# Moving the activation tiles of a decoder kernel by 64 bytes in on-chip memory

## The chip, the cores and the metric

The kernel runs on one core of one Trainium2 chip. The metric is the device time of one execution in microseconds (us). Three runs of the kernel before gave 1953.02, 1953.22 and 1953.27 us, a median of 1953.22.

## The reference

A decoder trunk of two layers, for 512 tokens of 1024 features in float32. Every sub-layer is wrapped in two norms: `x = x + w * norm(f(norm(x)))`, with `w` = 1/2 for the feed-forward sub-layers and 1 for the mixers.

```
ffn(h)   = (silu(h @ w_gate) * (h @ w_up)) @ w_down        # 1024 -> 2816 -> 1024, four times
conv(h)  = (b * causal_conv3(c * u)) @ w_out               # b, c, u = split(h @ w_in), layer 0
k, v     = split(norm(x) @ w_kv)                           # after layer 0
attn(h)  = norm((softmax(q1 k1) - lam * softmax(q2 k2)) v) @ w_o   # 8 heads, causal, layer 1
```

Layer 0 is ffn, conv, ffn; layer 1 is ffn, attn, ffn.

## The kernel before

Features lie on the 128 partitions, tokens along the free dimension; the residual stream `x` is one tile of 8 x 512 floats in each partition. All large products are made of three float32r matmuls (L128 to L130): weights and activations are each split into a high and a low part, and `hi*hi + hi*lo + lo*hi` is summed in PSUM.

```
nc.tensor.matmul(acc, wh, ah, start=first and j == 0, stop=False)
nc.tensor.matmul(acc, wh, al, start=False, stop=False)
nc.tensor.matmul(acc, wl, ah, start=False, stop=last and j == n - 1)
```

The second argument is the stationary operand, which TensorE loads first (LDWEIGHTS, 128 columns); the third is the moving operand, which it then streams. In the projections (`products`, called by `projects`) the weight part is stationary, 128 x 128, and the activation part is streamed: 512 columns for all tokens, or 256 for one half of the tokens. Halves are used around the end of a sub-layer (`closing` and the `head` of the next one), where the norm of one half runs while TensorE works on the other. In two places the roles are swapped: the last down projection (`ByTokens`, L339 to L341, sums named `d_acc`) and the values of attention (`values`, L567 to L569, sums named `v_acc`) hold 128 x 128 of an activation part still and stream 512 columns of a weight part. The scores of attention (L602) multiply tiles from the weight pools with each other: `pair_of_units("kq")` holds the parts of the queries and keys of one head.

A weight unit (`unit`, L107) is loaded by SyncE's queue into a `raw` tile of 4096 bytes per partition, ScalarE copies it to the high part `whi` (L113) and VectorE subtracts to get the low part `wlo` (L114). There are 2 raw tiles and 7 pairs of parts; units are prepared ahead and wait for a free pair.

Nothing in the kernel names an address. Memory of a partition is handed out to the pools in the order in which they are created, and within a pool to its tiles one after the other, each rounded up to 32 bytes. The pools that matter, with the start addresses of the built program, and what is left after dividing by 256:

| pool, in the order before | tiles, bytes per partition | start before, remainder | start after, remainder |
|---|---|---|---|
| `const` | 15 constants, 3136 together | 16512, 128 | 16512, 128 |
| `xpool` | the residual stream, 16384 | 19648, 192 | 19712, 0 |
| `apool` | 40 activation tiles, 2048 each | 36032, 192 | 36096, 0 |
| `mpool` | 2 large tiles, 8224 each (attention weights, conv) | 117952, 192 (second: 224) | 183552, 0 (second: 32) |
| `wraw` | 2 raw weight tiles, 4096 each | 134400, 0 | 175360, 0 |
| `wsp` | 7 + 7 weight parts, 4096 each | 142592, 0 | 118016, 0 |
| `tpool` | temporaries, 1024 and 2048 each | 199936, 0 | 200000, 64 |
| `rpool` | rows of the norms | 219008, 128 | 219072, 192 |

All slices that a matmul takes of an `apool` or `wsp` tile start at a multiple of 512 bytes from the tile's start, so they have the tile's remainder. Before, the streamed operand of a projection has the remainder 192 and the stationary one 0; in the swapped products it is the other way round.

Of the kernel before, what the change touches and what calls it, by code (L numbers as in the profile page):

```python
# [17 lines left out]
P = 128  # L18
# [5 lines left out]
NH = 8  # L24
HD = 64
EPS = 1e-6
CHUNKS = [(0, 7), (7, 14), (14, 22)]
LAST_CHUNKS = [(0, 8), (8, 16), (16, 22)]
HALVES = [(0, 256), (256, 512)]
# [13 lines left out]
def yoco_kernel(ctx: ExitStack, tc, i, out):  # L43
# [2 lines left out]
    const = ctx.enter_context(tc.tile_pool(name="const", bufs=1))  # L46
    xpool = ctx.enter_context(tc.tile_pool(name="xpool", bufs=1))
    apool = ctx.enter_context(tc.tile_pool(name="apool", bufs=5 * NK))
    mpool = ctx.enter_context(tc.tile_pool(name="mpool", bufs=1))
    wraw = ctx.enter_context(tc.tile_pool(name="wraw", bufs=RAW))  # L50
    wsp = ctx.enter_context(tc.tile_pool(name="wsp", bufs=WUNITS))
    tpool = ctx.enter_context(tc.tile_pool(name="tpool", bufs=1))
    small = ctx.enter_context(tc.tile_pool(name="small", bufs=4))
    rpool = ctx.enter_context(tc.tile_pool(name="rpool", bufs=1))
# [15 lines left out]
    ps = ctx.enter_context(tc.tile_pool(name="ps", bufs=6, space=PSUM))  # L70
    pst = ctx.enter_context(tc.tile_pool(name="pst", bufs=2, space=PSUM))

# [1 line left out]
    nc.scalar.preload_act_table_set("abs_reciprocal_sqrt_and_small")  # L74
    halves = {}
    for n in (D, 2 * HD):
# [10 lines left out]
    gsub = const.tile([P, 1], F32, name="gsub")  # L87
    nc.scalar.dma_start(gsub, i["gsub"])

# [1 line left out]
    x = xpool.tile([P, NK, S], F32, name="x")  # L91

    def load_x(k, n, t):
# [8 lines left out]
        return hi, lo  # L102

    def unit(src, n, pieces=1, between=lambda: None):
        """A stretch of weights and its two exact parts."""
        raw = wraw.tile([P, 1024], F32, tag="raw", name="raw")
        hi, lo = pair_of_units("w")  # L107
        for j in range(pieces):
            if j > 0:
                between()  # L110
            z = slice(j * n // pieces, (j + 1) * n // pieces)
            nc.sync.dma_start(raw[:, z], src[:, z])
            nc.scalar.copy(hi[:, z], raw[:, z])  # L113
            nc.vector.tensor_tensor(lo[:, z], raw[:, z], hi.bitcast(F32)[:, z], op=ALU.subtract)  # L114
        return hi, lo
# [6 lines left out]
        nc.vector.tensor_tensor(dst_lo, src, dst_hi.bitcast(F32), op=ALU.subtract)  # L122

    def products(acc, pairs, first=True, last=True):
        """acc (+)= sum of w.T @ a over (w_hi, w_lo, a_hi, a_lo)."""
        n = len(pairs)
        for j, (wh, wl, ah, al) in enumerate(pairs):
            nc.tensor.matmul(acc, wh, ah, start=first and j == 0, stop=False)  # L128
            nc.tensor.matmul(acc, wh, al, start=False, stop=False)  # L129
            nc.tensor.matmul(acc, wl, ah, start=False, stop=last and j == n - 1)  # L130
# [5 lines left out]
        return [ps.tile([P, S], F32, tag="ps", name="acc")[:, : t[1] - t[0]] for _ in us]  # L136

    def projects(us, h, t, accs=None, ks=None, nk=None):
        """One feature tile of a projection for the tokens t for each unit; each of h's tiles is used up in turn."""
        accs = accs or sums(us, t)  # L140
        for k in ks or range(len(h)):
            hh, hl = h[k]
            for u, acc in zip(us, accs):
                pair = cols(u, k) + (hh[:, t[0] : t[1]], hl[:, t[0] : t[1]])
                products(acc, [pair], k == 0, k == (nk or len(h)) - 1)
        return accs
# [1 line left out]
    def project(u, h, t):  # L148
        return projects([u], h, t)[0]

# [1 line left out]
    def inv_rms(total, dst, n, by_log=False):  # L152
        """dst = 1 / sqrt(v), v = mean + EPS, with one Newton step; total holds -mean / 2."""
        y = temp(n, "n_y")
        if by_log:
            nc.scalar.activation(y, total, AF.Ln, bias=eps, scale=-2.0)
            nc.scalar.activation(y, y, AF.Exp, scale=-0.5)
        else:
            nc.scalar.activation(y, total, AF.Abs_reciprocal_sqrt, bias=eps, scale=-2.0)
        q = temp(n, "n_q")  # L160
        nc.scalar.square(q, y)
        nc.vector.scalar_tensor_tensor(q, total, -0.5 * EPS, q, op0=ALU.add, op1=ALU.mult)
        nc.vector.scalar_tensor_tensor(dst, q, 1.5, y, op0=ALU.add, op1=ALU.mult)

    def squares_of(accs, src, m):
        """Adds tile m's squares to one of two sums."""
        acc = accs[m % 2]
        if m < 2:
            nc.scalar.square(acc, src)
        else:  # L170
            sq = temp(src.shape[-1], "sq")
            nc.scalar.square(sq, src)
            nc.vector.tensor_tensor(acc, acc, sq, op=ALU.add)
# [12 lines left out]
        return [parts_of("h") for _ in range(NK)]  # L186

    class Prenorm:
        """h = x * g in two parts, r2 = 1 / rms(x), for the tokens t: each tile's hi, lo, then the rest."""

        def __init__(self, gi):
            self.gi, self.h = gi, new_h()
# [23 lines left out]
            inv_rms(total_of(accs, b - a, a > 0), self.r2[:, a:b], b - a)  # L216

    def post(f, r1, c, t, after, ks=range(NK)):
        """x += c * f / rms(f), and what comes after on each tile of x."""
        a, b = t  # L220
        for k in ks:
            d = temp(b - a, "d")
            nc.vector.scalar_tensor_tensor(d, f[k][:, a:b], c[:, k : k + 1], r1, op0=ALU.mult, op1=ALU.mult)  # L223
            nc.vector.tensor_tensor(x[:, k, a:b], x[:, k, a:b], d, op=ALU.add)  # L224
            after.hi(k, t)
            if k > 0:
                after.lo(k - 1, t)
        if k == NK - 1:
            after.lo(k, t)
# [5 lines left out]
            pass  # L235

    def closing(groups, c, after, then, step=2):
        """The last projection of a sub-layer: groups(ms, t) gives those tiles' finished PSUM sums for the
        tokens t. Ends with the first half of the tokens ahead of the second: what follows on the first half
        (then) runs while the second's norms are under way."""  # L240
        f = [slot(F32, "f") if p is None else p for p in groups.parts]
        faccs = [rpool.tile([P, S], F32, tag=z, name=z) for z in ("facc0", "facc1")]

        def finish(ms, t):
            a, b = t
            for m, acc in zip(ms, groups(ms, t)):
                if groups.parts[m] is None:
                    nc.scalar.copy(f[m][:, a:b], acc)
                else:
                    nc.vector.tensor_tensor(f[m][:, a:b], f[m][:, a:b], acc, op=ALU.add)  # L250
                squares_of([z[:, a:b] for z in faccs], f[m][:, a:b], m)

        def rms(t):
            a, b = t
            for m in range(NK - TAIL, NK):
                finish([m], t)
            r1 = temp(b - a, "r1")
            inv_rms(total_of([z[:, a:b] for z in faccs], b - a, a == 0), r1, b - a)
            return r1

        for m in range(0, NK - TAIL, step):
            finish(range(m, m + step), FULL)
        one, two = HALVES
        post(f, rms(one), c, one, after)
        r1 = rms(two)
        ahead = then(one)
        next(ahead, None)
        after.rest(one)
        post(f, r1, c, two, after, range(POST_FIRST))
        next(ahead, None)  # L270
        post(f, r1, c, two, after, range(POST_FIRST, NK))
        run(ahead)
        after.rest(two)
        run(then(two))

    class Groups:
# [13 lines left out]
            return projects(us, self.a, t)  # L290

        def begin(self, m, ks):
            """Tile m's products over the tiles ks, ahead of the rest."""
            accs = self.begun[m][0] if m in self.begun else sums([m], FULL)
            projects([self.take(m)], self.a, FULL, accs, ks, NK)
            self.begun[m] = accs, range(ks[-1] + 1, NK)

    class ByTokens:
        """The last projection of the trunk with tokens on partitions: out = x + g / 2 * f / rms(f)."""

        def __init__(self, src):
            self.src = src
# [70 lines left out]
                self.f[tt, half, "s"] = slot(F32, "fg")  # L373
            return self.f[tt, half, "s"]

# [1 line left out]
    def ffn(l, s, h, pn, extra=None):  # L377
        r2 = pn.r2
        parts = [None] * NK
# [64 lines left out]
        return head, body  # L444

    def conv(l, h, pn):
        """z[t] = w0 cu[t-2] + w1 cu[t-1] + w2 cu[t], y = b z."""
        r2 = pn.r2
        rr = rpool.tile([P, S], F32, tag="rr", name="rr")
        y, us, cus = [], [], []  # L450
# [44 lines left out]
    def attention(l, h, pn, xkv):  # L495
# [10 lines left out]
        )  # L506
        gs = c.tile([P, 1], F32, name="gs")
        nc.vector.tensor_scalar_mul(gs, gsub, 1.0 - LAMBDA_INIT)
        # -lambda
        lam = temp(4 * HD, "lam")  # L510
        nc.scalar.dma_start(lam, i["lam"].broadcast_to([P, 4 * HD]))
        lprod = temp(2 * HD, "lprod")
# [25 lines left out]
        def body(after, then):  # L538
# [9 lines left out]
                    for k in range(3 * (n - 6), min(3 * (n - 6 + 1), NK) if n < NH - 2 else NK):  # L548
                        split(hkv[k][0], hkv[k][1], xkv[k])

# [1 line left out]
            v = {}  # L552

            vu = {}
# [33 lines left out]
                split(kq[n][0], kq[n][1], qs[n])  # L588

            def scores(n, qt):  # L590
                """mixed = softmax of the first component - lambda * softmax of the second."""
                qh, ql, kh, kl = kq[n]
                w = (qt + 1) * P
                qq = slice(qt * P, w)
# [21 lines left out]
                mixed[n, qt] = e[0]  # L616

            def block(z, j, qt):
                """Keys of tile j, queries of tiles qt on (qt >= j), of a head's transposed weights."""
                return z[:, (3 * j + qt) * P : (3 * j + NB) * P]  # L620

            def turn(n, qt):
# [77 lines left out]

        return head, body

# [1 line left out]
    xkv = []  # L704

    def keep():
        """x * g_kv / rms(x), which the keys and values come from."""
        for _ in range(2):
            z = large(F32, "xkv")
            xkv.extend(z[:, k, :S] for k in range(4))  # L710
# [37 lines left out]


def _tiles(w):  # L750
    """(K, M) -> (M/128, 128, K/128 * 128): each 128 columns' stationary tiles side by side."""
    k, m = w.shape
    return w.reshape(k // P, P, m // P, P).transpose(2, 1, 0, 3).reshape(m // P, P, k)


def _cols(v):
    """(..., 1024) -> (128, ..., 8): features on partitions."""
    import numpy as np

    return np.moveaxis(v.reshape(*v.shape[:-1], NK, P), -1, 0)  # L760
# [42 lines left out]
```

## Time and profile before

| quantity | value |
|---|---|
| median of the runs | 1953.22 us |
| span of the profiled execution (first to last instruction) | 1951.1 us |
| TensorE busy | 1929.1 us, 99% |
| weight loads busy (beside the matmuls) | 1599.9 us, 82% |
| VectorE busy | 993.6 us, 51% |
| ScalarE busy | 737.6 us, 38% |
| bytes moved by DMA | 178.45 MB, 91 GB/s |

The profile comes from one execution; of it the span is known, 2.1 us below the median of the runs. A busy matmul overlaps the next one, so TensorE's busy time doesn't tell how close together matmuls start: that is read from the starts in the timeline. In the groups, `acc<-h_lo,whi 128*128 128x512 f32 x1376` means 1376 matmuls that write a sum `acc` from the streamed tile `h_lo` and the stationary tile `whi`, 128 x 128 weights, 512 columns (the two inputs are named in no fixed order); after the bar stand the busy time, the mean duration in ns, and the idle time before them. Lines of the timeline begin with the start and the duration in us.

### The profile page before, as it was taken

The page shows a single profiled execution, that of the slowest core. Times are in us where ns is not written, and L with a number is a line of the kernel's source. Part 1 is how long each engine was busy: PE and PEld are TensorE (multiplying, and loading weights), DVE is VectorE, ACT ScalarE, POOL GpSimd, SP SyncE. Part 2 cuts the span into 40 slices and gives each one's busy share as a digit, 9 for nine tenths or more (in the row PEclk, how much of TensorE's full clock was granted, in tenths as well). Part 3 has the DMA queues.
Part 4 walks back from the last instruction along what each step waited for, and adds up shares of the span by engine and source line. Part 5 has one row for each costly group of instructions (what it writes and reads, how often), then busy time and mean ns, then how long its engine had stood idle before and what let it go on. Part 6 is the DMA issues. An engine that isn't in the chain of part 4 may idle for free.

```text
span 1951.1 us, 24217 instructions
## 1 busy us (share of the span) xinstructions
PE 1929.1 (99%) x9762; PEld 1599.9 (82%) x9762; DVE 993.6 (51%) x1666; ACT 737.6 (38%) x1243; POOL 1.1 (0%) x8
## 2 busy tenths in 40 slices
PE   8999999999999999999999999999999999999998
PEld 8888888988898888888988888899866898878886
DVE  6424434574566334344862433358389594244345
ACT  6332223352345322222632222245289663332132
POOL 0000000000000000000000000000000000000000
PEclk9999999999999999999999999999999999999999
DMA  4323322222223323233133232222211223223221
GB/s 161 112 98 100 99 92 86 87 87 97 99 85 102 101 89 91 94 98 97 54 113 107 90 105 94 90 87 84 68 44 56 75 67 129 83 90 102 93 87 65
DMA packets 52655, 178.45 MB, mean 91 GB/s; under 512 B 6208, under 2 KB 8384, under 8 KB 52544
## 3 DMA queue, kind: packets, MB, share of 16 engines
q1 hardware_dynamic: 51536, 176.18, 27.8%
q8 instruction: 77, 1.26, 0.3%
q10 hardware_dynamic: 1008, 0.72, 0.1%
q14 instruction: 34, 0.28, 0.0%
HBM read 174.79 MB, written 2.10 MB: 91 GB/s over the span
## 4 chain that ended last, share of the span: by engine, by line
PE 88%; DVE 7%; ACT 3%; DMA 1%; issue 1%; SPq 0%; DVEq 0%; ACTq 0%
PE acc L130 26%; PE acc L129 26%; PE acc L128 26%; PE d_acc L340 2%; PE d_acc L341 2%; PE d_acc L339 2%; DVE d L223 1%; DVE h_lo L202 1%; DVE x L224 1%; DVE wlo L114 1%; PE v_acc L569 1%; PE v_acc L568 1%; PE v_acc L567 1%; ACT e L610 1%; DVE top L605 1%
## 5 line engine op out<-in xcount | busy, mean ns | idle before, releaser
L128 PE MATMUL acc<-h_hi,whi 128*128 128x512 f32 (+1 forms) x1952 | 706.7, 363 | 7.5 <-ACT whi L113 7.1
L130 PE MATMUL acc<-h_hi,wlo 128*128 128x512 f32 (+1 forms) x1952 | 706.4, 362 | 0.4 <-DVE wlo L114 0.4
L129 PE MATMUL acc<-h_lo,whi 128*128 128x512 f32 (+1 forms) x1952 | 706.6, 362 | 0.2
L113 ACT CAST whi<-raw 128x1024 fp32r<-128x1024 f32 (+2 forms) x335 | 337.7, 1032 | 904.4 <-PE acc L129 744.5
L114 DVE TENSOR_TENSOR wlo<-raw,whi 128x1024 fp32r<-128x1024 f32 (+2 forms) x335 | 400.5, 1198 | 246.7 <-ACT whi L113 245.9
L128 PEld LDWEIGHTS acc<-h_hi,whi 128*128 128x128 f32 x1952 | 368.0, 189 | 71.5 <-ACT whi L113 7.6
L130 PEld LDWEIGHTS acc<-h_hi,wlo 128*128 128x128 f32 x1952 | 368.0, 189 | 63.8 <-DVE wlo L114 1.1
L129 PEld LDWEIGHTS acc<-h_lo,whi 128*128 128x128 f32 x1952 | 368.3, 189 | 63.2 <-DVE h_lo L202 0.8
L388 DVE TENSOR_TENSOR gs<-acc,r 128x512 f32<-128x512 f32 (+1 forms) x100 | 62.5, 625 | 468.7 <-PE acc L130 468.4
L129 PE MATMUL acc<-act_lo,whi 128*128 128x512 f32 (+1 forms) x624 | 224.8, 360 | 0.0
L130 PE MATMUL acc<-act_hi,wlo 128*128 128x512 f32 (+1 forms) x624 | 224.2, 359 | 0.0
L128 PE MATMUL acc<-act_hi,whi 128*128 128x512 f32 (+1 forms) x624 | 224.2, 359 | 0.0
L129 PEld LDWEIGHTS acc<-act_lo,whi 128*128 128x128 f32 x624 | 117.6, 188 | 19.8
L128 PEld LDWEIGHTS acc<-act_hi,whi 128*128 128x128 f32 x624 | 117.3, 188 | 19.7
L130 PEld LDWEIGHTS acc<-act_hi,wlo 128*128 128x128 f32 x624 | 117.3, 188 | 19.6
L119 ACT CAST act_hi<-us 128x512 fp32r<-128x512 f32 (+1 forms) x100 | 56.6, 569 | 67.4 <-DVE us L392 67.4
L341 PE MATMUL d_acc<-wlo,act_hi 128*128 128x512 f32 x176 | 69.4, 395 | 0.0
L340 PE MATMUL d_acc<-whi,act_lo 128*128 128x512 f32 x176 | 69.2, 394 | 0.0
L339 PE MATMUL d_acc<-whi,act_hi 128*128 128x512 f32 x176 | 68.8, 392 | 0.0
L390 DVE TENSOR_TENSOR us<-acc,r 128x512 f32<-128x512 f32 (+1 forms) x100 | 62.5, 625 | 1.4 <-PE acc L130 0.7
L122 DVE TENSOR_TENSOR act_lo<-us,act_hi 128x512 fp32r<-128x512 f32 (+1 forms) x100 | 61.7, 620 | 1.2 <-ACT act_hi L119 1.2
L392 DVE TENSOR_TENSOR us<-us,gs 128x512 f32<-128x512 f32 (+1 forms) x100 | 61.7, 620 | 0.3
(152 smaller groups left out, 1629.9 us busy)
## 6 DMA issues: line engine op xcount, KB each, us to landing
raw<-in_wu SPq DMA_DIRECT2D x88, 512.0 KB, 3.4
raw<-in_wg SPq DMA_DIRECT2D x87, 512.0 KB, 3.9
raw<-in_wd SPq DMA_DIRECT2D x48, 448.0 KB, 3.3
raw<-in_wd SPq DMA_DIRECT2D x24, 512.0 KB, 3.9
raw<-in_wci SPq DMA_DIRECT2D x24, 512.0 KB, 3.4
raw<-in_wdt SPq DMA_DIRECT2D x22, 512.0 KB, 3.6
raw<-in_wco SPq DMA_DIRECT2D x8, 512.0 KB, 3.4
raw<-in_wq SPq DMA_DIRECT2D x8, 512.0 KB, 3.5
```

The lines of the kernel that those rows point to most:

```text
L113: nc.scalar.copy(hi[:, z], raw[:, z])
L114: nc.vector.tensor_tensor(lo[:, z], raw[:, z], hi.bitcast(F32)[:, z], op=ALU.subtract)
L122: nc.vector.tensor_tensor(dst_lo, src, dst_hi.bitcast(F32), op=ALU.subtract)
L128: nc.tensor.matmul(acc, wh, ah, start=first and j == 0, stop=False)
L129: nc.tensor.matmul(acc, wh, al, start=False, stop=False)
L130: nc.tensor.matmul(acc, wl, ah, start=False, stop=last and j == n - 1)
L339: nc.tensor.matmul(acc, ah, wh, start=k == 0, stop=False)
L340: nc.tensor.matmul(acc, al, wh, start=False, stop=False)
L341: nc.tensor.matmul(acc, ah, wl, start=False, stop=k == m1 - m0 - 1)
L388: nc.vector.tensor_tensor(gs, g, r2[:, p:q], op=ALU.mult)
L390: nc.vector.tensor_tensor(us, up, r2[:, p:q], op=ALU.mult)
L392: nc.vector.tensor_tensor(us, us, gs, op=ALU.mult)
```

## The change

A constant tile `line` of 16 floats (64 bytes) is added ahead of all others; nothing writes or reads it. The pools `wsp` and `wraw` are created before `mpool`, whose two tiles together are 64 bytes more than a multiple of 256, and in the order `wsp`, `wraw`. The other lines of the diff take out comments.

```
+LINE = 16
...
     apool = ctx.enter_context(tc.tile_pool(name="apool", bufs=5 * NK))
+    wsp = ctx.enter_context(tc.tile_pool(name="wsp", bufs=WUNITS))
+    wraw = ctx.enter_context(tc.tile_pool(name="wraw", bufs=RAW))
     mpool = ctx.enter_context(tc.tile_pool(name="mpool", bufs=1))
-    wraw = ctx.enter_context(tc.tile_pool(name="wraw", bufs=RAW))
-    wsp = ctx.enter_context(tc.tile_pool(name="wsp", bufs=WUNITS))
...
+    const.tile([P, LINE], F32, name="line")
     nc.scalar.preload_act_table_set("abs_reciprocal_sqrt_and_small")
```

The instructions of all five engines, their order and the semaphores that they wait for are the same in both programs, row for row, apart from the numbers in tile names. What differs is the addresses in the table above.

## The prediction

> **What bounds the kernel now.** I read the page first: span, busy times, the shares of the chain that ended last. Then the span and clock of the core, the waits, the groups of TensorE's instructions with shapes kept apart, and the timeline at five places.
>
> ```profile
> span 1951.1 us, 24217 instructions
> PE 1929.1 (99%) x9762; PEld 1599.9 (82%) x9762; DVE 993.6 (51%) x1666; ACT 737.6 (38%) x1243; POOL 1.1 (0%) x8
> PE 88%; DVE 7%; ACT 3%; DMA 1%; issue 1%; SPq 0%; DVEq 0%; ACTq 0%
> core 0: 1951.1 us, clock 0.998
> ACT whi L113 <- PE acc L129: 744.5, 129, 9.5
> ```
>
> TensorE is busy for 99% of the span, it is 88% of the chain, and its clock is full (0.998). The other engines wait for it: ScalarE's split of the next weights (L113) stood 744.5 us in 129 waits until TensorE gave a weight buffer back. So the time is the number of matmuls times the step from one start to the next, and that step is the only quantity on which a change of addresses can act at this scale. The counts come from the groups. Each product has three matmuls of equal count (L128, L129, L130); of some I quote one row of the three.
>
> ```profile
> L129 PE MATMUL acc<-h_lo,whi 128*128 128x512 f32 x1376 | 544.3, 396 | 0.0
> L130 PE MATMUL acc<-act_hi,wlo 128*128 128x512 f32 x432 | 170.9, 396 | 0.0
> L129 PE MATMUL k_acc<-h_lo,whi 128*128 128x512 f32 x64 | 25.4, 396 | 0.0
> L129 PE MATMUL acc<-y_lo,whi 128*128 128x512 f32 x32 | 12.7, 396 | 0.0
> L129 PE MATMUL acc<-on_lo,whi 128*128 128x512 f32 x32 | 12.6, 395 | 0.0
> L129 PE MATMUL acc<-h_lo,whi 128*128 128x256 f32 x576 | 162.3, 283 | 0.2
> L129 PE MATMUL acc<-act_lo,whi 128*128 128x256 f32 x192 | 53.9, 281 | 0.0
> L129 PE MATMUL acc<-y_lo,whi 128*128 128x256 f32 x64 | 17.7, 276 | 0.0
> L129 PE MATMUL acc<-on_lo,whi 128*128 128x256 f32 x64 | 17.7, 276 | 0.0
> L341 PE MATMUL d_acc<-wlo,act_hi 128*128 128x512 f32 x176 | 69.4, 395 | 0.0
> L569 PE MATMUL v_acc<-wlo,h_hi 128*128 128x512 f32 x64 | 25.2, 394 | 0.0
> ```
>
> **Wide** matmuls (512 columns) that stream an activation tile against a stationary weight: 3 x (1376 + 432 + 64 + 32 + 32) = 5808. **Narrow** ones (256 columns): 3 x (576 + 192 + 64 + 64) = 2688. **Swapped** ones, which stream the weights and hold the activation still: 3 x (176 + 64) = 720.
>
> The column of durations is no price: durations overlap (396 ns each, while starts lie closer). The step is read from starts. First the wide ones, in the middle of a feed-forward layer (nine steps from the first row to the last):
>
> ```profile
> 699.82 0.39 PE L130 MATMUL acc<-h_hi,wlo 128*128 128x512 f32 x1
> 700.05 0.40 PE L128 MATMUL acc<-h_hi,whi 128*128 128x512 f32 x1
> ...
> 701.69 0.39 PE L129 MATMUL acc<-h_lo,whi 128*128 128x512 f32 x1
> 701.92 0.40 PE L130 MATMUL acc<-h_hi,wlo 128*128 128x512 f32 x1
> ```
>
> (701.92 - 699.82) / 9 = 233.3 ns. 5808 of them are 1355 us, 69% of the span.
>
> **The change part by part.** *Instructions.* Nothing is added, removed or reordered on any engine, and every semaphore wait stands where it stood; the new constant tile is never written. No step is moved past a queue. What changes is addresses: the activation tiles go from 192 to 0 above a multiple of 256 bytes, the weight parts stay on multiples of 256. So of the two operands it is the activation that moves: the streamed one in the wide and narrow matmuls, the stationary one in the swapped ones.
>
> *Wide matmuls, the term of the sum.* Before has a class of products with the same 512 columns whose streamed operand already lies on a multiple of 256: the swapped ones, which stream weights. Their stationary operand lies 192 above. Their steps, in two places of the last projection (again nine steps each):
>
> ```profile
> 1679.79 0.39 PE L341 MATMUL d_acc<-wlo,act_hi 128*128 128x512 f32 x1
> 1680.02 0.39 PE L339 MATMUL d_acc<-whi,act_hi 128*128 128x512 f32 x1
> ...
> 1681.62 0.39 PE L340 MATMUL d_acc<-whi,act_lo 128*128 128x512 f32 x1
> 1681.85 0.39 PE L341 MATMUL d_acc<-wlo,act_hi 128*128 128x512 f32 x1
> ```
>
> ```profile
> 1819.65 0.40 PE L339 MATMUL d_acc<-whi,act_hi 128*128 128x512 f32 x1
> 1819.89 0.40 PE L340 MATMUL d_acc<-whi,act_lo 128*128 128x512 f32 x1
> ...
> 1821.52 0.40 PE L341 MATMUL d_acc<-wlo,act_hi 128*128 128x512 f32 x1
> 1821.75 0.40 PE L339 MATMUL d_acc<-whi,act_hi 128*128 128x512 f32 x1
> ```
>
> The first is 2.06 / 9 = 228.9 ns, 4.4 ns shorter than the wide ones; the second is 2.10 / 9 = 233.3 ns, the same as the wide ones, with the same remainders of its addresses. So there is a faster pace that I have seen only where the streamed operand is on a multiple of 256, but such an operand does not guarantee it. The paces repeat without drift over many steps, so I read them as a stream that falls into step with something (the weight load that runs beside it, most likely); alignment would then change which steady paces exist, and the start of a stretch which one is taken. Taking the fast pace for all wide matmuls: 5808 x 4.4 ns = 25.6 us less. Bounds: nothing, if all fall into the slow pace; and 51 us, if the stationary operand's alignment is worth a second step of the same size. I take 25.6, since the row at 228.9 ns is nearest in shape, type and streamed address; the term is on the path whole, because the waits show the others ahead of TensorE (VectorE at 51%, ScalarE at 38%), and they have 1.3% less time for the same work.
>
> [...]
>
> *Narrow matmuls.* They too have two paces, and here at one and the same alignment:
>
> ```profile
> 594.77 0.28 PE L129 MATMUL acc<-h_lo,whi 128*128 128x256 f32 x1
> 594.88 0.28 PE L130 MATMUL acc<-h_hi,wlo 128*128 128x256 f32 x1
> ...
> 595.79 0.28 PE L129 MATMUL acc<-h_lo,whi 128*128 128x256 f32 x1
> ```
>
> ```profile
> 35.83 0.28 PE L130 MATMUL acc<-h_hi,wlo 128*128 128x256 f32 x1
> 35.95 0.28 PE L128 MATMUL acc<-h_hi,whi 128*128 128x256 f32 x1
> ...
> 36.89 0.28 PE L130 MATMUL acc<-h_hi,wlo 128*128 128x256 f32 x1
> ```
>
> 1.02 / 9 = 113.3 ns and 1.06 / 9 = 117.8 ns. Twice 113.3 is 226.6, below the wide step, so these are likely held by something other than the stream. All 2688 from one pace to the other would be 12 us; with both paces present already the change is worth less, to either side. I take 0 and keep 6 us each way for the range.
>
> *Swapped matmuls.* Their streamed operand stays, their stationary one moves to a multiple of 256. Bounds: 720 x 4.4 = 3.2 us either way; I take 0, since no row shows what a stationary address is worth.
>
> *Everything else.* VectorE's and ScalarE's tiles move by 64 bytes as well (the temporaries from 0 to 64, the norm's rows from 128 to 192). They are 10% of the chain, 195 us; no row prices this, a 1% change of all would be 2 us either way, and I take 0. One of the two tiles of transposed attention weights stays off the multiples (224 to 32); it takes part in at most 8 heads x 4 tiles x 3 = 96 matmuls, under 1 us at 4.4 ns each.
>
> The sum: -25.6 us. The profiled execution's span is 1951.1 us, 2.1 us under the median of the runs, 1953.2; I subtract from the median, as what lies around the span does not change: **1927.6 us**.
>
> **The rivals.**
>
> *No change: the change does nothing to the pace.* The place at 1820 us speaks for it: streamed operand on a multiple of 256, and still 233.3 ns. So would it be if only the start of a stretch picks the pace and the long projections pick the slow one, as the quoted stretch does. The time stays at 1953, within about 1.
> [...] Against it stands that 228.9 ns was seen at all, and only in the class whose streamed operand lies otherwise.
>
> *Slower: both operands at the same place collide.* In the wide products of before the two operands have different remainders; in the swapped ones too. After, all are equal, so the weight load and the stream start on the same bytes of a 256-byte span, and if memory serves them in turn they would meet more often. The only products of before with both on multiples of 256 are the scores of attention, in half-height matmuls:
>
> ```profile
> L602 PE MATMUL sc<-kqlo,kqhi 64*128 64x512 f32 x16 | 3.9, 406 | 0.0
> L602 PE MATMUL sc<-kqhi,kqlo 64*128 64x512 f32 x16 | 3.7, 391 | 0.0
> ```
>
> Their mean, 398.5 ns, is 2.5 to 3 above the wide ones' 396 where starts and durations differ by a fixed amount; two run at once there, which may be the whole reason. With 2.7 ns: 5808 x 2.7 = 16 us; the swapped ones lose the fast pace where they have it, at most 720 x 4.4 = 3 us. That gives 1953.2 + 19 = 1972. It decides as soon as a wide step is above 233.3.
>
> *Much faster: the stationary address counts as well.* Then wide 224.5 and swapped 224.5 where they had 228.9: 51 + 3 = 54 us, 1899. For it: the idea that each operand off its multiple costs one more access. Against: a narrow step, which has the same load, is no longer for it.
>
> **How the numbers follow.** Forecast 0.47; much faster 0.13; no change 0.18; slower 0.22. The forecast leads because it is the one that a row of the right shape shows; slower is more than a remote case because both operands have never stood at the same place in full-height products. A measurement of this kernel tells about 0.2%, 4 us, from no change. Faster by more than that: 0.47 + 0.13 = 0.60; within: 0.18; slower: 0.22. The forecast's own range is 1918 (6 us of the narrow and 3 of the swapped ones gained too) to 1940 (a quarter of the wide ones in the slow pace, 6 us, and 6 us lost by the narrow ones). The range for 8 in 10 goes down to 1897, which takes in most of much faster, and up to 1962, which takes in no change and the smaller half of slower; left out are the rest of slower and gains over 56 us, some 0.18.
>
> **What would show it.** In the timeline of the changed kernel at a feed-forward projection, nine steps of wide matmuls: 2.06 us if right, 2.10 if nothing changed, over 2.12 if they collide, near 2.02 if the stationary operand counts. The groups should show the 396 of `acc` fall to about 392, and the narrow ones unmoved. TensorE stays at 99% and the waits keep their order. Wrong it would be if the wide step is unchanged or longer, or if the time moves while that step does not: then a wait took over that the page of before hides.

## The result, and the profile after

The changed kernel takes 1920.30 us (median of 4 runs, 1919.03 to 1920.53), the kernel before 1953.24 us beside it: a ratio of 0.983, 95% interval 0.9816 to 0.9844, 33 us faster. The page and the core's row of the changed kernel:

```profile
span 1918.0 us, 24217 instructions
PE 1898.9 (99%) x9762; PEld 1610.0 (84%) x9762; DVE 993.5 (52%) x1666; ACT 737.7 (38%) x1243; POOL 1.1 (0%) x8
PE 92%; DVE 4%; ACT 2%; DMA 1%; issue 0%; DVEq 0%; SPq 0%; ACTq 0%
core 0: 1918.0 us, clock 0.999
```

TensorE is still busy for 99% and leads the chain (92% where it was 88%). VectorE and ScalarE have the same busy times as before to 0.1 us, so moving their tiles by 64 bytes cost nothing. What is shorter lies between the starts of matmuls. The timeline of the changed kernel, nine steps each of wide, narrow and swapped matmuls (start and duration in us first; L131 to L133 are L128 to L130 of before, L342 to L344 are L339 to L341):

```profile
582.85 0.28 PE L133 MATMUL acc<-h_hi,wlo 128*128 128x256 f32 x1
582.97 0.28 PE L131 MATMUL acc<-h_hi,whi 128*128 128x256 f32 x1
...
583.93 0.28 PE L133 MATMUL acc<-h_hi,wlo 128*128 128x256 f32 x1
...
699.75 0.39 PE L133 MATMUL acc<-h_hi,wlo 128*128 128x512 f32 x1
699.98 0.39 PE L131 MATMUL acc<-h_hi,whi 128*128 128x512 f32 x1
...
701.79 0.39 PE L133 MATMUL acc<-h_hi,wlo 128*128 128x512 f32 x1
...
1789.93 0.39 PE L344 MATMUL d_acc<-wlo,act_hi 128*128 128x512 f32 x1
1790.16 0.39 PE L342 MATMUL d_acc<-whi,act_hi 128*128 128x512 f32 x1
...
1791.97 0.39 PE L344 MATMUL d_acc<-wlo,act_hi 128*128 128x512 f32 x1
```

Wide: 2.04 / 9 = 226.7 ns where it was 233.3. Swapped: 226.7 ns, also in the middle third of the last projection, where it was 233.3. Narrow: 1.08 / 9 = 120.0 ns, longer than either pace of before (113.3 and 117.8). The groups show the same in the durations:

```profile
L132 PE MATMUL acc<-h_lo,whi 128*128 128x512 f32 x1376 | 536.0, 390 | 0.0
L132 PE MATMUL acc<-h_lo,whi 128*128 128x256 f32 x576 | 164.5, 287 | 0.0
L342 PE MATMUL d_acc<-whi,act_hi 128*128 128x512 f32 x176 | 68.4, 390 | 0.0
```

390 for 396 in the wide ones, 287 for 283 in the narrow ones. Summing the distances from each start to the next over both traces, each put down to the matmul that starts it, gives the account of the 33 us by class (differences taken before rounding):

| class of matmul | sum before, us | sum after, us | difference | steady step before and after, ns |
|---|---|---|---|---|
| wide | 1362.2 | 1324.8 | -37.4 | 233.3, 226.8 |
| narrow | 329.0 | 336.2 | +7.2 | 115.0, 119.9 |
| swapped | 165.6 | 163.2 | -2.4 | 230.2, 226.7 |
| others | 81.0 | 80.9 | -0.2 | |

A steady step is one under 125 ns (narrow) or 242 ns (the others). The narrow ones lose more in their steady steps (+14.4 us, 297.7 to 312.1) than in all: their longer steps, in which TensorE waits, fell from 31.4 to 24.1 us. So about half of what the slower pace costs is time in which TensorE would have waited anyway.

### The profile page after: what moved, and what is told of

Its sections match the earlier page's. It is cut to its first block, busy times and chain, and to the rows that moved or that the text cites. A ratio compares the mean times of both kernels' runs of the same rounds, so it can differ in the third digit from the quotient of the medians.

```text
span 1918.0 us, 24217 instructions
## 1 busy us (share of the span) xinstructions
PE 1898.9 (99%) x9762; PEld 1610.0 (84%) x9762; DVE 993.5 (52%) x1666; ACT 737.7 (38%) x1243; POOL 1.1 (0%) x8
## 4 chain that ended last, share of the span: by engine, by line
PE 92%; DVE 4%; ACT 2%; DMA 1%; issue 0%; DVEq 0%; SPq 0%; ACTq 0%
PE acc L133 27%; PE acc L131 27%; PE acc L132 27%; PE d_acc L343 2%; PE d_acc L342 2%; PE d_acc L344 2%; PE v_acc L570 1%; PE v_acc L571 1%; PE v_acc L572 1%; ACT e L613 1%; DVE top L608 1%; DMA raw<-in_wg 1%; DVE wlo L117 1%; PE tot L185 1%; ACT whi L116 1%
## 5 line engine op out<-in xcount | busy, mean ns | idle before, releaser
L131 PE MATMUL acc<-h_hi,whi 128*128 128x512 f32 (+1 forms) x1952 | 701.0, 360 | 7.5 <-ACT whi L116 7.4
L133 PE MATMUL acc<-h_hi,wlo 128*128 128x512 f32 (+1 forms) x1952 | 701.0, 360 | 0.0
L116 ACT CAST whi<-raw 128x1024 fp32r<-128x1024 f32 (+2 forms) x335 | 337.8, 1032 | 871.2 <-PE acc L132 741.1
L131 PEld LDWEIGHTS acc<-h_hi,whi 128*128 128x128 f32 x1952 | 369.5, 190 | 62.2 <-ACT whi L116 7.9
L133 PEld LDWEIGHTS acc<-h_hi,wlo 128*128 128x128 f32 x1952 | 369.9, 190 | 54.7 <-DVE wlo L117 0.9
L133 PE MATMUL acc<-act_hi,wlo 128*128 128x512 f32 (+1 forms) x624 | 222.6, 357 | 0.0
L131 PE MATMUL acc<-act_hi,whi 128*128 128x512 f32 (+1 forms) x624 | 222.6, 357 | 0.0
L131 PEld LDWEIGHTS acc<-act_hi,whi 128*128 128x128 f32 x624 | 118.0, 189 | 16.9
L133 PEld LDWEIGHTS acc<-act_hi,wlo 128*128 128x128 f32 x624 | 118.0, 189 | 16.6
L342 PE MATMUL d_acc<-whi,act_hi 128*128 128x512 f32 x176 | 68.4, 390 | 0.0
L344 PE MATMUL d_acc<-wlo,act_hi 128*128 128x512 f32 x176 | 68.4, 389 | 0.0
```

What stands on the lines that cost most here:

```text
L342: nc.tensor.matmul(acc, ah, wh, start=k == 0, stop=False)
L344: nc.tensor.matmul(acc, ah, wl, start=False, stop=k == m1 - m0 - 1)
```

## The experiments

Two theories beside the one on record (the streamed operand's own alignment): that each operand counts by itself, and that the distance between the two counts, whatever their place. Before, the streamed operand of a projection is 192 ahead of the stationary one (modulo 256), in the swapped products 64; after, 0 in both. The three runs that only time matmuls were executed once each.

### The two halves of the change, and a map of addresses

The first run leaves the kernel out and only measures matmuls (the comments are added here):

```
+    for n in (S, S // 2):
+        for s in STATIONARY:          # a..h: 0, 32, ... 224
+            for m in MOVING:
+                stretch(m, s, n)      # 42 matmuls at these two places
```

> Leaves all of the computation out but one kind of product: triples of matmuls (high weight with high and low activation, low weight with high activation) on fixed data, 42 matmuls for each pair of a streamed and a stationary address, both at 0, 32, ... 224 above a multiple of 256 bytes; first all 64 pairs with 512 columns, then all with 256. The steps of before and after should come back: 226.7 ns wide and 120.0 narrow at 0 and 0, 233.3 wide and 113.3 or 117.8 narrow at 192 streamed and 0 stationary, 228.9 or 233.3 wide at 0 and 192. If only the streamed address counts, the step is the same for all stationary addresses of a streamed one. If only the difference of the two counts, it is the same for all pairs of equal difference, so 226.7 wide for all eight equal pairs. If each operand off its multiple costs by itself, 0 and 0 is the fastest wide pair and every other is slower.

The timeline of this run, nine steps each: the streamed operand at 192 and the stationary at 0 (`wide_mg_sa`), the reverse (`wide_ma_sg`), and both at 192 (`wide_mg_sg`):

```profile
76.74 0.39 PE L72 MATMUL wide_mg_sa<-buf 128*128 128x512 f32 x1
76.97 0.39 PE L70 MATMUL wide_mg_sa<-buf 128*128 128x512 f32 x1
...
78.84 0.39 PE L72 MATMUL wide_mg_sa<-buf 128*128 128x512 f32 x1
...
485.72 0.39 PE L70 MATMUL wide_ma_sg<-buf 128*128 128x512 f32 x1
485.95 0.39 PE L71 MATMUL wide_ma_sg<-buf 128*128 128x512 f32 x1
...
487.78 0.39 PE L70 MATMUL wide_ma_sg<-buf 128*128 128x512 f32 x1
...
545.04 0.39 PE L70 MATMUL wide_mg_sg<-buf 128*128 128x512 f32 x1
545.27 0.39 PE L71 MATMUL wide_mg_sg<-buf 128*128 128x512 f32 x1
...
547.08 0.39 PE L70 MATMUL wide_mg_sg<-buf 128*128 128x512 f32 x1
```

2.10 / 9 = 233.3, 2.06 / 9 = 228.9 and 2.04 / 9 = 226.7 ns: the three wide paces of the two kernels, here with TensorE alone at work but for a copy of each sum. The whole map, as the mean of the last 30 steps of each stretch from the starts in the trace, in ns (rows: streamed operand at 0, 32, ... 224; columns: stationary operand):

```
wide        0     32     64     96    128    160    192    224
  0     226.8  233.3  233.3  234.2  233.3  233.3  228.9  233.3
 32     233.3  226.7  233.3  233.3  234.3  232.3  233.3  228.9
 64     228.9  233.3  226.7  233.3  233.3  234.3  233.3  233.3
...
192     233.3  234.3  233.3  233.3  228.9  233.3  226.7  233.3
224     233.3  233.3  234.3  233.3  233.3  228.9  233.3  226.7
narrow
  0     120.0  118.2  117.8  118.7  118.7  120.0  117.8  117.8
 32     117.8  120.0  118.2  113.3  117.3  118.7  120.0  117.8
```

The wide rows are nearly one row shifted: what counts is the distance. All eight equal pairs run at 226.7 or 226.8, all eight with the stream 64 ahead at 228.9, nearly all others at 233.3 to 234.3. Equal places are the slowest of this map for narrow matmuls, 120.0 in all eight (one of several distances with that pace); a distance of 192 gives 113.3 or 117.8.

The second run has the padding alone (the line of `const`, with the pools in the order before), so activations lie at 0 and weights at 64.

> Half of the change: the padding of the constants without the new order of the pools. Activations lie on multiples of 256, weight parts 64 above. If only the streamed address counts: wide steps 226.7 ns and narrow ones 120.0 as after, time about 1920. If the difference of the two addresses counts: it is 192 modulo 256 in the projections, as before, so 233.3 ns wide and about 1953. If each operand counts by itself: wide between the two, 1925 to 1945.

The third has the new order of the pools alone (the change without the tile `line`), so both lie at 192.

> The other half: the new order of the pools without the padding. Activations and weight parts both lie 192 above multiples of 256. If only the streamed address counts: wide steps 233.3 ns, time about 1953. If the difference of the two counts: it is 0 as after, 226.7 ns and about 1920. If each operand counts by itself, both are off their multiples and wide steps are the longest, 233.3 or more: 1953 to 1975.

Padding alone: 1953.45 us, a ratio of 0.9999 to before (0.999 to 1.0009). Order alone: 1920.20 us, 0.9831 (0.9816 to 0.9846), as the whole change. The timelines in a feed-forward layer, first of the padding alone, then of the order alone:

```profile
699.75 0.39 PE L133 MATMUL acc<-h_hi,wlo 128*128 128x512 f32 x1
699.99 0.39 PE L131 MATMUL acc<-h_hi,whi 128*128 128x512 f32 x1
...
701.85 0.39 PE L133 MATMUL acc<-h_hi,wlo 128*128 128x512 f32 x1
```

```profile
699.93 0.39 PE L133 MATMUL acc<-h_hi,wlo 128*128 128x512 f32 x1
700.16 0.39 PE L131 MATMUL acc<-h_hi,whi 128*128 128x512 f32 x1
...
701.97 0.39 PE L133 MATMUL acc<-h_hi,wlo 128*128 128x512 f32 x1
```

2.10 / 9 = 233.3 and 2.04 / 9 = 226.7 ns. With the streamed operand on a multiple of 256 and a distance of 192 nothing is gained; with neither operand on a multiple and a distance of 0, everything. The first two theories fall; the third holds in all three runs.

### Finer distances, half a weight load, bfloat16

```
+AHEAD = dict(zip("abcdefghijklmnopq",
+    (0, 8, 16, 24, 32, 48, 64, 128, 192, 208, 224, 232, 240, 248, 256, 512, 1024)))
+            for d in AHEAD:
+                stretch(kind, d, n)
+                if r:
+                    other(r)                       # 1 or 2 matmuls of 384 columns
+    for d in "agi":
+        stretch("thin", d, S, cols=P // 2)         # half a weight load
+    for d in "aghi":
+        stretch("short", d, S, z=buf16)            # bfloat16
```

> Leaves all of the computation out but triples of matmuls on fixed data, 36 for each distance of the streamed operand ahead of the stationary one: 0 to 32 and 192 to 256 bytes in steps of 8 or 16, then 512 and 1024; each three times, and in the second and third time after one or two matmuls of 384 columns, so that a stretch starts otherwise. If the distance modulo 256 decides: 226.7 ns wide and 120.0 narrow at 0, 256, 512 and 1024, and 113.3 or 117.8 narrow at 192, whichever the start leaves. At the end 512 columns against half a weight load (64 columns), and in bfloat16, at distances of 0, 64, 128 and 192. If the step above the streaming itself comes from the weight load beside it, half a load costs less than a whole one and the distance matters less; in bfloat16, with half the bytes, the step would hardly depend on the distance. If it came from the stream's own crossing of some boundary, half a load would change nothing.

Steps in ns by distance, from the starts of the last 19 matmuls of each stretch, at the three starts (11 of the 17 distances):

```
bytes      0       8      16      24      64     192     240     248     256     512    1024
wide   226.7   233.3   232.0   233.3   228.9   233.3   236.7   230.0   226.7   226.7   226.7
       226.7   233.3   232.0   233.3   233.3   233.3   236.7   230.0   226.7   226.7   226.7
       226.6   233.3   231.8   233.5   228.9   233.3   236.7   230.0   226.7   226.7   226.7
narrow 120.1   126.7   116.7   120.0   113.3   113.3   116.9   120.0   120.0   120.0   120.0
       120.0   120.0   118.6   120.0   117.8   113.3   117.2   120.0   120.0   120.0   120.0
       120.0   120.0   118.7   120.0   117.8   117.8   117.1   120.0   120.1   120.0   120.0
```

256, 512 and 1024 are like 0 (226.7 wide, 120.0 narrow), as a period of 256 would have it. Of all distances tried, equal places are the best for wide matmuls; a stream 8 bytes ahead loses the whole gain (233.3), one 8 bytes behind (248) half of it (230.0). At a distance of 64, wide (228.9 and 233.3), and of 8 (126.7 and 120.0), 64 and 192 (113.3 and 117.8), narrow, one distance shows two paces in the three rounds. The rounds differ in what runs just before a stretch, so the start seems to pick the pace; what in it does so is not isolated. It fits the last projection of before, whose middle third ran at 233.3 ns and the other two at 228.9, and the two paces of the narrow ones. Half a weight load and bfloat16, both at a distance of 0, in the timeline:

```profile
679.71 0.39 PE L71 MATMUL thin_da<-buf 128*64 128x512 f32 x1
679.94 0.40 PE L72 MATMUL thin_da<-buf 128*64 128x512 f32 x1
...
682.47 0.39 PE L71 MATMUL thin_da<-buf 128*64 128x512 f32 x1
...
703.42 0.38 PE L72 MATMUL short_da<-buf_short 128*128 128x512 bf16 x1
703.64 0.38 PE L70 MATMUL short_da<-buf_short 128*128 128x512 bf16 x1
...
705.15 0.38 PE L71 MATMUL short_da<-buf_short 128*128 128x512 bf16 x1
```

Half a load: 2.76 us for twelve steps, 230.0 ns, not less than the whole load's 226.7. At 64 it takes 228.3 and at 192 232.8, where the whole load takes 228.9 or 233.3, and 233.3. So that half a load costs less, as I expected, does not hold; that the distance matters less does (4.5 ns between the best and the worst of the three, for 6.6). bfloat16: 1.73 us for eight, 216 ns, and 215.8 in its steady steps at all four distances, 10.9 under the float32r products at their best (226.7). So the dependence is seen with float32r and not with bfloat16; whether the bytes or the type decide is not shown.

### Which two reads meet

```
+PAIRS = {"equal": (0, 0, 0, 0), "own": (0, 128, 0, 128), "next": (0, 128, 128, 0), "apart": (0, 0, 128, 128)}
+        for j in range(count):
+            nc.tensor.matmul(acc, still[j % 2], streamed[j % 2], start=j == 0, stop=j == count - 1)
```

> Leaves all of the computation out but stretches of 36 matmuls, each three times, that alternate between two streamed and two stationary tiles. equal: all four on multiples of 256 bytes. apart: both stationary ones 128 above. own: the second matmul's streamed and stationary tile both 128 above, so each matmul's own two operands are at distance 0 and each stream is 128 from the stationary operand of the matmul that follows. next: the reverse, own operands 128 apart, each stream at distance 0 from the next matmul's stationary operand. Equal gives 226.7 ns wide and 120.0 narrow, apart 233 wide. If a stream meets the weight load of the next matmul, next is like equal and own like apart. If a matmul's own operands matter, own is like equal and next like apart. If the load partner is neither, or two streams in a row matter, both differ from equal.

From the starts (last 20 steps): wide 226.7 equal, 228.3 own, 230.0 next, 232.4 apart; narrow 120.0, 116.7, 116.7, 118.7. The groups, whose first one holds the start of the run:

```profile
L69 PE MATMUL wide_equal<-buf 128*128 128x512 f32 x108 | 27.3, 414 | 14.0 <-ACT buf L57 14.0
L69 PE MATMUL wide_apart<-buf 128*128 128x512 f32 x108 | 25.6, 395 | 0.0
L69 PE MATMUL wide_next<-buf 128*128 128x512 f32 x108 | 25.3, 392 | 0.0
L69 PE MATMUL wide_own<-buf 128*128 128x512 f32 x108 | 25.2, 391 | 0.0
```

Neither of the two simple answers holds: both mixed cases lie between equal and apart when wide, and below both when narrow. Two streams in a row are 128 apart in both, which may count as well. Which reads meet stays open.

### Narrow matmuls at their own distance

Weights that only narrow matmuls use can be placed 64 bytes further on, at a distance of 192. Tiles of 4352 bytes make room for it; two half-size temporaries and one full-size one pay.

```
-HALF_TEMPS = 10
+HALF_TEMPS = 8
-TEMPS = 4
+TEMPS = 3
+SHIFT = 16
-        hi = wsp.tile([P, 1024], F32R, tag="whi", name=name + "hi")
+        hi = wsp.tile([P, 1088], F32R, tag="whi", name=name + "hi")
...
+        return hi[:, off : off + 1024], lo[:, off : off + 1024]
...
-            us.extend(load(m, *(cut if m == 0 else ())) for m in range(HEAD_PAIRS))
+            us.extend(load(m, *(cut if m == 0 else ()), off=SHIFT) for m in range(HEAD_PAIRS))
```

(and so in the other heads and the last four units of each closing). The twin has `SHIFT = 0`.

> The change, with 64 bytes more in front of the weights that only narrow matmuls use (heads of sub-layers and the last four tiles of a closing projection), so that wide products have a distance of 0 and narrow ones of 192; each weight tile takes 4352 bytes, and two of ten half-size temporaries and one of four full-size ones are given up for it. If the distance decides each product by itself: wide 226.7 ns, narrow 113.3 to 117.8 where after has 119.9, so 2688 times 2 to 6.5 ns, 6 to 18 us under the run without the shift. If the padding's place in memory matters in some other way, no difference between the two.

> The same kernel without the shift: larger weight tiles and fewer temporaries, all distances 0. Wide 226.7, narrow 119.9 ns as after; the fewer temporaries may cost a few us, so 1920 to 1930.

1919.68 us (1918.96 to 1922.96) with the shift, 1922.93 (1921.88 to 1924.77) without: their ranges overlap, so this pair is inconclusive. The twin is 2.6 us above the changed kernel, perhaps for the missing temporaries. A second pair keeps all full-size temporaries:

```
-TEMPS = 3
+TEMPS = 4
-        rr = rpool.tile([P, S], F32, tag="rr", name="rr")
+        rr = rpool.tile([P, S], F32, tag="facc1", name="rr")
```

> The narrow shift again, with all four full-size temporaries kept and only two half-size ones given up; the convolution's row of 2048 bytes shares a place with a sum of the closing norm. Narrow 116.4 ns on average as in the run before, wide 226.8. If that run lost its gain to the missing temporaries: about 1912. If the shorter narrow steps only turn into waits for the norms: 1917 to 1920.

> The same without the shift. About 1920 as after; the difference to the run with the shift is what the shift is worth here: 8 to 12 us if the narrow steps count in full, 3 or less if they turn into waits.

1916.83 us (1915.55 to 1917.42, 5 runs) against 1921.12 (1920.50 to 1921.94, 4 runs): 4.3 us, and no run of the one lies in the range of the other. Against before the ratios are 0.9811 (0.9797 to 0.9824) and 0.9834 (0.982 to 0.9847). The timeline of the run with the shift:

```profile
582.80 0.28 PE L132 MATMUL acc<-h_hi,whi 128*128 128x256 f32 x1
582.91 0.28 PE L133 MATMUL acc<-h_lo,whi 128*128 128x256 f32 x1
...
583.82 0.28 PE L132 MATMUL acc<-h_hi,whi 128*128 128x256 f32 x1
```

1.02 / 9 = 113.3 ns here; over the trace the steady steps are 116.0 on average and 226.9 for the wide ones. The steady narrow steps sum to 299.9 us where the twin has 312.4, 12.5 less, but the longer ones to 31.3 where it has 23.5, 7.8 more, and 4.7 us are left: most of the gain turns into waits. Of the 7.8 us, 4.3 stand directly before the norms' sums `tot` (7.0 us of longer steps, 2.7 in the twin). So the 4.3 us between the medians lie between the two cases expected, 8 to 12 and 3 or less. This version has the lowest median of all and is clearly faster than before; its interval overlaps with that of the change as it was made (ratio 0.983).

## Why the prediction came out, and where it was wrong

*What bounds the kernel* was right: TensorE's steps, and nothing hidden took over. A gain of 37.4 us in the wide steps arrived in the time whole; the preparation of the weight units stayed ahead (ScalarE's split waited 741.1 us for TensorE, where it was 744.5, and TensorE 7.4 us for the split, where it was 7.1).

*Wide matmuls* were mis-sized: 4.4 ns a step on record, 6.6 measured, -37.4 us in place of -25.6. The reason given failed. I took the streamed operand's alignment to be the cause, from the swapped products, and the padding alone shows that it is worth nothing (233.3 ns). What ran at 228.9 there was a distance of 64, and the change does not go to that distance but to 0, of which before had no full-height row. So the row nearest in shape and streamed address was the wrong neighbour. That the time still fell in the range, 7.3 us under the 1927.6 forecast, is in part luck: by the reason given, the padding alone would have brought the 25.6 us, and the gain came because the change also puts the two operands at the same place. What did hold is that the steady paces change with the addresses (233.3 ns at a distance of 192, 226.7 at 0), and that one distance can have two (228.9 and 233.3 ns at 64).

*Narrow matmuls* were put at 0, 6 us each way; they cost 7.2. The step that failed is that with both paces present already the change would be worth nothing: their pace depends on the distance as well, with an order of its own (113.3 or 117.8 ns at 192), and 0 is among their worst (120.0 ns). Whether something other than the stream holds them, as the prediction supposed, is not shown. *Swapped*: 0 on record, within 3.2; measured -2.4. The rest was 0, as priced.

*The rivals.* "Both operands at the same place collide" had the right variable, equal remainders, and the wrong sign: equal is best for wide matmuls (226.7 ns). The half-height scores that supported it were no guide. The narrow ones did get slower at equal places, which the rival did not price. "No change" was right that the place at 1820 us shows a second pace at the same addresses; it missed that at a distance of 0 the wide ones showed only one pace, 226.7 ns, the same at all three starts. "Much faster" had the stationary operand count by itself, which the order alone refutes (226.7 ns with neither operand on a multiple).

## What to carry to other kernels

Where float32r matmuls with a weight load each run back to back, look at where the streamed and the stationary operand lie relative to each other modulo 256 bytes, and read the step from starts, not from busy time: here 512-column steps were shortest at equal places (226.7 ns), 256-column steps at a distance of 64 or 192 (113.3 or 117.8 ns, where equal places took 120.0). A chain of pools decides that distance, and an odd-sized pool between the two is enough to set it; an experiment that moves both operands tells relative from absolute. A product of one shape that runs faster elsewhere in the kernel is evidence for a pace, not for its cause.

## What was not expected of the hardware

- A step depended on the distance between the two operands, down to 8 bytes: wide 226.7 to 236.7 ns, narrow 113.3 to 126.7, in runs where TensorE alone works but for a copy of each sum. It was the same at 0, 256, 512 and 1024 bytes (226.7 wide, 120.0 narrow). By an estimate from these steps, the commonest paces are multiples of 6.67 ns (226.7 is 34 times it, 233.3 is 35, 120.0 is 18, 113.3 is 17) or lie at a third of it between two (228.9, 117.8); others, such as 234.3, do not fit. Why is not known.
- At some distances two paces were seen, and how a stretch starts seems to pick one: 228.9 or 233.3 wide at 64, 113.3 or 117.8 narrow at 192.
- Half a weight load was not cheaper than a whole one (230.0 against 226.7 ns at a distance of 0; 232.8 against 233.3 at 192).
